# A two-layer hybrid backbone on one Trainium2 core: the state-space part's last step is emitted within the output projection, and its decay rows are asked for two steps ahead

## The chip, the cores and the metric

One NeuronCore of a Trainium2 chip runs the whole program in one launch. The metric is the device time of that core in microseconds, lower is better; beside the timed runs there is one profiled execution, from which every row below is taken.

## The reference

Two layers work on 512 latent tokens and 256 context tokens of width 1024. In each, a modulated RMS norm and an input projection feed three parallel mixers: latent attention, retention and a state-space mixer (SSD). Their outputs, side by side, go through one output projection; then comes a dense feed-forward part (layer 0) or a router with eight experts (layer 1). The last layer gives only the latent tokens. What the change touches is the state-space mixer, for each of 8 heads and both directions:

```
acum = cumsum(log_a)                       # per chunk of 128 tokens
seg = acum[:, None] - acum[None, :]
decay = exp(where(mask, seg, -inf))
scores = (q k^T) * decay
y = scores v                               # within the chunk
state = state * exp(acum[-1]) + (k * w_end)^T v
y += (q * exp(acum)) state_in              # from the chunks before
y = rmsnorm((y + xs * d_skip) * silu(z))
out = concat(att, ret, y) @ w_out
```

## The kernel before, in words

The kernel is written for a tile framework: Python code emits instructions, a scheduler sorts them by priority (the order in which they were emitted, as far as dependences and free buffers let it), and each of the five engines then runs its own list strictly in that order. Tiles come from pools with a fixed number of slots, set in `open_main` (L263): `s2` has 23 slots of 2 KB a partition, `s3` has 30 of 3 KB, `b1` has 4 PSUM tiles of one bank, `w` holds four weight tiles `wraw` of 512 KB each with their high and low parts `whi` and `wlo`. All weight and row transfers are issued by SP, one after the other; an issue waits on SP until its tile is free, and what stands behind it waits too.

The state-space part of a layer is the generator `ssd_run` (L761). It first runs `ssd_states` (L718): the cumulative sums go to DRAM (`cumd`, L725), the chunk states are made (`csps`) and passed on in a scan (`scan_step`, tiles `cs`), with the retention mixer's transposes (`mid`) in between. Then it loops over steps. A step is one chunk of 128 tokens and one of two groups of four heads; layer 0 has 6 chunks, so 12 steps, in the order of chunks 4, 5, 0, 1, 2, 3 (the context first); layer 1 has 4 chunks and 8 steps. For a step,

- `spread` (L780) asks for the decay rows: two transfers (one a direction) of four rows of `cumd`, each copied to all 128 partitions, into two `segE` tiles of `s2`;
- `seg` (L787) subtracts the column sums: eight ScalarE activations of 128x128, four into a PSUM tile `segps` and four in place in `segE`, and VectorE merges them with one predicated copy (L795);
- `weights` (L798) takes the exponential on ScalarE and multiplies with the scores `smask` on VectorE;
- `out` (L803) makes four products `ssdy` on TensorE into the chunk's PSUM tile, eight records in the profile;
- `scores` (L765) for each chunk makes `smask` and the coefficients `cf`; `inter` (L810) for each chunk makes the products `ssdi` with the incoming state, scaled on VectorE (`ssdt`) and added on GpSimd (`ssdu`);
- `final` (L829) adds up a finished chunk and multiplies with the gate `z` (two VectorE operations on `ssdu`); `done` (L1441) takes its square sum on ScalarE, and for every pair of chunks a chain of small VectorE operations (`rq_f`) makes the reciprocal root that scales the pair.

In the loop (L838 to L855) iteration i asks for the rows of step i+1, subtracts for step i, makes the weights of step i-1 and the products of step i-2. The rows of the first step are asked for when the scan is done.

`weave` (L88) emits this generator interleaved with two others by weights: the modulation columns and gates (`mods`: loads `wraw<-in_modw_dram`, products `modps`) and the gate z (`z_run`: products `zps`). The weight of the state-space generator is 22.6 + 5.3 for each chunk (L1457). Behind the weave, `mix_T` (L985) transposes finished chunks by pairs into the projection's operands (`mixps` on TensorE, `mixh` on ScalarE, `mixl` on VectorE), and `wout` (L1464) makes the output projection: for each half of the columns and each 128-token tile 24 products `woutps` (8 slices of the inner dimension, each with three split products) into one `b1` tile, then `x`: a product with the gate and a sum with the residual `xre`. The transposes of the last pair of chunks are emitted within the first half, ahead of the last tile but one (`late`, L1482). What follows is the norm, the feed-forward part (`ffn`, whose `hh`, `hl` and tanh tile `fth` are `s3` tiles like the 16 tiles of its input) or the router and the experts.

Of the kernel before, what the change touches and what calls it, by code (L numbers as in the profile page):

```python
# [255 lines left out]
class Net:  # L256
# [5 lines left out]

    def open_main(self, w=(4, 4, 4), s3=30, s2=23, b2=2, b1=4):  # L263
        tc, ctx = self.tc, self.ctx
# [452 lines left out]

    def ssd_states(self, l, xsT, bmT, mid):  # L718
        pr = self.b2("rowps")
# [20 lines left out]
        yield 5.2  # L740
        yield from mid()
        for cs_, steps in self.SCAN:
            PS = {}
# [17 lines left out]
    def ssd_run(self, l, order, xsT, bmT, cmT, Z, mid, done):  # L761
        IN = yield from self.ssd_states(l, xsT, bmT, mid)
        Wt, SMs, py, fin, R, cf = {}, {}, {}, {}, {}, {}
# [72 lines left out]
        steps = [(c, g) for c in order for g in range(2)]  # L836
        spread(*steps[0])
        scores(order[0])  # L838
        for i, (c, g) in enumerate(steps):
            if i + 1 < len(steps):  # L840
                spread(*steps[i + 1])
            seg(c, g)
            if i:
                weights(*steps[i - 1])
            if g == 1 and i + 1 < len(steps):
                scores(steps[i + 1][0])
            yield 1.0
            if i >= 2:
                out(*steps[i - 2])
                if steps[i - 2][1]:  # L850
                    final(steps[i - 2][0])
                yield 0.9
            if g == 1:
                inter(c)
                yield 0.9  # L855
# [490 lines left out]
    def mixer(self, l, hT, begin, mods, last):  # L1346
# [39 lines left out]
        mixT = self.new_T("mix", 2)  # L1386
# [65 lines left out]
        def late(tl):  # L1452
# [3 lines left out]
        Z = {}  # L1456
        weave((self.ssd_run(l, out_t, xsT, bmT, cmT, Z, ret_mix, done), 22.6 + 5.3 * len(out_t)), (mods, 0.5 if last else 20.0),  # L1457
              (self.z_run(l, hT, out_t, Z), 6.5 * len(out_t)))
        mixT.extend(self.new_T("mix", 4))
        for tl in segt[:-1]:  # L1460
            late(tl)()
        return mixT, late(segt[-1])

    def wout(self, l, mixT, tiles, gates, xin, late, hook, mid=None):  # L1464
# [9 lines left out]
        for h in range(2):  # L1474
# [4 lines left out]
            for i, t in enumerate(tiles):  # L1479
                n = h * len(tiles) + i  # L1480
                load(n + 2)
                if h == 0 and i == len(tiles) - 2:  # L1482
                    late()
                s = 0 if t < 4 else 1
                cs = slice(128 * t, 128 * t + 128)
                ps = self.b1("woutps")
                for k in range(8):
                    o = 512 * (k % 2)
                    self.mm3(ps, (mixT[k][0][:, cs], mixT[k][1][:, cs]),
                             (us[k // 2][0][:, o:o + 512], us[k // 2][1][:, o:o + 512]), k == 0, k == 7)  # L1490
                    if mid and k in (1, 4, 5):
                        mid()
# [704 lines left out]
```

## Time and profile before

| | |
|---|---|
| median of 3 runs | 2031.25 us (2030.02 to 2034.23) |
| the profiled execution | 2027.31 us, its span 2025.5 us |
| mean granted clock of TensorE | 0.965 of full speed |
| TensorE busy | 1888.1 us |
| the state-space stretch of layer 0 | about 355 to 425 us of the span |
| the state-space stretch of layer 1 | about 1320 to 1360 us of the span |

The span is from the first to the last instruction; the execution's own time is 1.8 us more. The engines work side by side, so the busy times don't add up to the span: what counts is which engine stands still in a stretch, and for whom. In the rows, PE is TensorE, PEld its loading of weights, DVE VectorE, ACT ScalarE, POOL GpSimd, SP the engine that issues most transfers. A name like `ssdy<-xst,segE` gives the tile written and those read.

### The profile page before, as it was taken

How to read it: one execution, taken by the hardware profiler on the slowest of the kernel's cores; microseconds unless marked ns; L12 is line 12 of the kernel's file. 1: busy time of each engine (PE TensorE's matmuls, PEld its weight loads, DVE VectorE, ACT ScalarE, POOL GpSimd, SP SyncE). 2: the span in 40 equal slices, each digit the busy share in tenths (PEclk: the TensorE clock that was granted, in tenths of full speed). 3: DMA queues.
4: the chain of work that ended last, by engine and by line, in shares of the span. 5: the costliest groups of instructions: out<-in, count | busy, mean ns of one | idle time of the engine just before them, and what ended most of it. 6: DMA issues, size and time to landing. Idle time of an engine off the chain costs nothing. (4 is left out here: it accounts for less than half of the span.)

```text
span 2025.5 us, 28080 instructions
## 1 busy us (share of the span) xinstructions
PE 1888.1 (93%) x10467; PEld 1549.7 (77%) x10467; DVE 1252.4 (62%) x2470; ACT 832.9 (41%) x1400; POOL 241.7 (12%) x220
## 2 busy tenths in 40 slices
PE   5999999879999999999999999979699889989896
PEld 3777886668888888888887778867588768877774
DVE  5555374667733933833677455775786679659875
ACT  4444223734321220221244442363464467447654
POOL 1100011310003003003002000231210211011001
PEclk9999999989999999999998999979799989999998
DMA  6401115623422711711722011233995799569952
GB/s 242 147 24 35 42 58 193 224 84 105 139 80 70 243 63 53 249 63 61 230 74 88 22 42 63 65 119 116 364 373 172 231 332 335 191 189 364 348 158 72
DMA packets 103208, 310.06 MB, mean 153 GB/s; under 512 B 12171, under 2 KB 19467, under 8 KB 103008
## 3 DMA queue, kind: packets, MB, share of 16 engines
q1 hardware_dynamic: 96320, 290.96, 41.7%
q0 software_dynamic: 6272, 16.43, 2.9%
q8 instruction: 102, 1.67, 0.3%
q14 instruction: 98, 0.80, 0.1%
q10 hardware_dynamic: 416, 0.20, 0.0%
HBM read 293.86 MB, written 14.94 MB: 152 GB/s over the span
## 5 line engine op out<-in xcount | busy, mean ns | idle before, releaser
L309 DVE TENSOR_TENSOR ws<-wr,ws 128x1024 fp32r<-128x1024 f32 (+1 forms) x272 | 319.7, 1191 | 140.2 <-ACT ws L306 120.9
L321 PE MATMUL gups<-ws,xT 128*128 128x512 f32 (+1 forms) x1536 | 349.3, 387 | 26.7 <-issue 18.9
L306 ACT ACTIVATE ws<-wr 128x1024 fp32r<-128x1024 f32 (+1 forms) x272 | 278.8, 1032 | 185.9 <-PE gups L321 106.1
L321 PEld LDWEIGHTS gups<-ws,xT 128*128 128x128 f32 x1536 | 274.6, 192 | 89.1 <-issue 29.0
L306 ACT ACTIVATE whi<-wraw 128x1024 fp32r<-128x1024 f32 x126 | 133.1, 1057 | 493.5 <-PE downps L321 127.7
L309 DVE TENSOR_TENSOR wlo<-wraw,whi 128x1024 fp32r<-128x1024 f32 x123 | 152.8, 1244 | 148.4 <-ACT whi L306 147.7
L321 PE MATMUL dnps<-ws,hTh 128*128 128x512 f32 (+1 forms) x484 | 151.4, 400 | 0.0
L321 PE MATMUL gps<-mixh,whi 128*128 128x256 f32 (+1 forms) x360 | 120.9, 336 | 3.0 <-DVE fth L318 3.0
L321 PE MATMUL gps<-mixl,whi 128*128 128x256 f32 (+1 forms) x360 | 120.9, 336 | 1.2 <-POOL mixl L309 0.7
L321 PE MATMUL gps<-mixh,wlo 128*128 128x256 f32 (+1 forms) x360 | 120.2, 334 | 0.0
L321 PE MATMUL ups<-mixl,whi 128*128 128x256 f32 (+1 forms) x360 | 119.9, 333 | 0.0
L321 PE MATMUL ups<-mixh,whi 128*128 128x256 f32 (+1 forms) x360 | 119.8, 333 | 0.0
L321 PE MATMUL ups<-mixh,wlo 128*128 128x256 f32 (+1 forms) x360 | 119.7, 332 | 0.0
L318 DVE SCALAR_TENSOR_TENSOR junk<-wraw,crow 128x512 bf16<-128x512 f32 x160 | 104.9, 706 | 10.5 <-DMA wraw<-in_modw_dram 10.5
L321 PE MATMUL downps<-whi,hh 128*128 128x512 f32 x264 | 103.7, 393 | 2.0 <-DVE nv L315 2.0
L321 PEld LDWEIGHTS dnps<-ws,hTh 128*128 128x128 f32 (+1 forms) x484 | 88.1, 186 | 21.0
L321 PE MATMUL downps<-wlo,hh 128*128 128x512 f32 x264 | 103.4, 392 | 0.0
L321 PE MATMUL downps<-whi,hl 128*128 128x512 f32 x264 | 103.2, 391 | 0.0
L1955 POOL DMA_INDIRECT yd<-my,dst x20 | 42.6, 2128 | 490.8 <-DVE my L318 463.6
L309 POOL TENSOR_TENSOR x<-x,dtmp 128x512 f32<-128x512 f32 x36 | 50.2, 1396 | 390.0 <-DVE dtmp L309 390.0
L309 DVE TENSOR_TENSOR dtmp<-downps,gate 128x512 f32<-128x512 f32 x48 | 33.0, 690 | 95.2 <-PE downps L321 86.3
L321 PE MATMUL dnps<-ws,hTl 128*128 128x512 f32 x220 | 87.5, 398 | 0.0
(410 smaller groups left out, 4076.7 us busy)
## 6 DMA issues: line engine op xcount, KB each, us to landing
wr<-in_moe_dram SPq DMA_DIRECT2D x248, 512.0 KB, 5.4
wraw<-in_modw_dram SPq DMA_DIRECT2D x94, 512.0 KB, 4.0
wraw<-in_ffn_dram SPq DMA_DIRECT2D x66, 512.0 KB, 3.8
wraw<-in_win_dram SPq DMA_DIRECT2D x44, 512.0 KB, 3.3
segE<-cumd SPq DMA_DIRECT2D x40, 256.0 KB, 4.3
wraw<-in_wout_dram SPq DMA_DIRECT2D x16, 512.0 KB, 3.5
wr<-in_moe_dram POOLq DMA_DIRECT2D x8, 512.0 KB, 15.8
wr<-in_moe_dram SPq DMA_DIRECT2D x16, 256.0 KB, 3.4
```

Of the source, the lines that this page charges most:

```text
L306: return self.nc.scalar.activation(out, in_, func, **kw)
L309: return (eng or self.nc.vector).tensor_tensor(out, a, b, op)
L318: return self.nc.vector.scalar_tensor_tensor(out, a, s, b, op0, op1, accum_out=accum)
L321: return self.nc.tensor.matmul(out, lhsT, rhs, start=start, stop=stop)
L1955: nc.gpsimd.indirect_dma_start(out=self.yd[h], out_offset=bass.IndirectOffsetOnAxis(ap=self.dst[:r, c:c + 1], axis=0), in_=y[b][h][:r], in ...
```

## The change

- `ssd_states` takes a callback that asks for the rows of the first two steps once the retention transposes are emitted, ahead of the scan; in the loop, iteration i asks for the rows of step i+2.
- `inter` of a chunk is emitted at its first step and no longer at its second.
- The generator yields None ahead of its last iteration, and the weave runs it only up to there, with the weight 22.6 + 4.8 for each chunk - 3.0. `mixer` hands the generator on, and `wout` advances it after the third and the sixth slice of each of the first tiles of its first half, and to its end ahead of the last pair's transposes. So the last step's subtraction, the last two steps' weights and products and the last chunk's `final` are emitted between products of the projection.
- `s3` has 29 slots, `s2` has 26.

```diff
--- before.py
+++ after.py
@@ -260,7 +260,7 @@
         self.dp = ctx.enter_context(tc.tile_pool(name="dram", bufs=1, space=DRAM))
         self.zero_made = False
 
-    def open_main(self, w=(4, 4, 4), s3=30, s2=23, b2=2, b1=4):
+    def open_main(self, w=(4, 4, 4), s3=29, s2=26, b2=2, b1=4):
         tc, ctx = self.tc, self.ctx
         self.pools = ExitStack()
         self.cp = self.pools.enter_context(tc.tile_pool(name="cst", bufs=1))
@@ -715,7 +715,7 @@
         i = o.index(c) + 1
         return o[i] if i < 6 else None
 
-    def ssd_states(self, l, xsT, bmT, mid):
+    def ssd_states(self, l, xsT, bmT, mid, spread):
         pr = self.b2("rowps")
         for c in range(6):
             self.tr(pr[:16, 128 * c:128 * c + 128], self.cumS[:, c, :])
@@ -739,6 +739,7 @@
             self.act(self.xst[c], ps)
         yield 5.2
         yield from mid()
+        spread()
         for cs_, steps in self.SCAN:
             PS = {}
             for c in cs_:
@@ -759,7 +760,6 @@
         return IN
 
     def ssd_run(self, l, order, xsT, bmT, cmT, Z, mid, done):
-        IN = yield from self.ssd_states(l, xsT, bmT, mid)
         Wt, SMs, py, fin, R, cf = {}, {}, {}, {}, {}, {}
         later = self.U.bitcast(I32).unsqueeze(1).to_broadcast([128, 4, 128])
 
@@ -834,11 +834,13 @@
             done(c, v)
 
         steps = [(c, g) for c in order for g in range(2)]
-        spread(*steps[0])
+        IN = yield from self.ssd_states(l, xsT, bmT, mid, lambda: [spread(*s) for s in steps[:2]])
         scores(order[0])
         for i, (c, g) in enumerate(steps):
-            if i + 1 < len(steps):
-                spread(*steps[i + 1])
+            if i == len(steps) - 1:
+                yield None
+            if i + 2 < len(steps):
+                spread(*steps[i + 2])
             seg(c, g)
             if i:
                 weights(*steps[i - 1])
@@ -850,7 +852,7 @@
                 if steps[i - 2][1]:
                     final(steps[i - 2][0])
                 yield 0.9
-            if g == 1:
+            if g == 0:
                 inter(c)
                 yield 0.9
         weights(*steps[-1])
@@ -1454,12 +1456,13 @@
         self.g2 = {}
         mods = cat(self.mod_gate(l, 2, (0,) if last else (0, 1), self.g2), *mods)
         Z = {}
-        weave((self.ssd_run(l, out_t, xsT, bmT, cmT, Z, ret_mix, done), 22.6 + 5.3 * len(out_t)), (mods, 0.5 if last else 20.0),
+        ssd = self.ssd_run(l, out_t, xsT, bmT, cmT, Z, ret_mix, done)
+        weave((iter(lambda: next(ssd), None), 22.6 + 4.8 * len(out_t) - 3.0), (mods, 0.5 if last else 20.0),
               (self.z_run(l, hT, out_t, Z), 6.5 * len(out_t)))
         mixT.extend(self.new_T("mix", 4))
         for tl in segt[:-1]:
             late(tl)()
-        return mixT, late(segt[-1])
+        return mixT, (ssd, late(segt[-1]))
 
     def wout(self, l, mixT, tiles, gates, xin, late, hook, mid=None):
         X = {t: [None, None] for t in tiles}
@@ -1480,7 +1483,9 @@
                 n = h * len(tiles) + i
                 load(n + 2)
                 if h == 0 and i == len(tiles) - 2:
-                    late()
+                    for _ in late[0]:
+                        pass
+                    late[1]()
                 s = 0 if t < 4 else 1
                 cs = slice(128 * t, 128 * t + 128)
                 ps = self.b1("woutps")
@@ -1488,6 +1493,8 @@
                     o = 512 * (k % 2)
                     self.mm3(ps, (mixT[k][0][:, cs], mixT[k][1][:, cs]),
                              (us[k // 2][0][:, o:o + 512], us[k // 2][1][:, o:o + 512]), k == 0, k == 7)
+                    if h == 0 and i < len(tiles) - 2 and k % 3 == 2:
+                        next(late[0], None)
                     if mid and k in (1, 4, 5):
                         mid()
                 x = self.s2("x")
```

The orders of the engines differ in the two state-space stretches alone. Three places of layer 0, each before and after (numbers are positions in the engine's list, `x` is a count of equal neighbours, line numbers of the changed kernel are up to 7 higher at the end):

SP, from the first load behind `cumd` on; `segE` are decay rows, two transfers a step, `wraw` the modulation and projection weights. Before:

```order
34 L376 DMA wraw<-in_modw_dram 128x1024 x7
35 L513 DMA gate<-modd_3118 128x4x128 x4
36 L376 DMA wraw<-in_modw_dram 128x1024 x4
37 L785 DMA segE<-cumd_2835 128x512 x6
38 L376 DMA wraw<-in_modw_dram 128x1024 x3
39 L785 DMA segE<-cumd_2835 128x512 x4
40 L376 DMA wraw<-in_modw_dram 128x1024 x3
41 L785 DMA segE<-cumd_2835 128x512 x4
42 L376 DMA wraw<-in_wout_dram 128x1024 x3
43 L785 DMA segE<-cumd_2835 128x512 x4
```

After:

```order
34 L376 DMA wraw<-in_modw_dram 128x1024 x3
35 L785 DMA segE<-cumd_2835 128x512 x4
36 L376 DMA wraw<-in_modw_dram 128x1024 x3
37 L513 DMA gate<-modd_3109 128x4x128 x4
38 L376 DMA wraw<-in_modw_dram 128x1024 x8
39 L785 DMA segE<-cumd_2835 128x512 x4
40 L376 DMA wraw<-in_modw_dram 128x1024
41 L785 DMA segE<-cumd_2835 128x512 x2
42 L376 DMA wraw<-in_modw_dram 128x1024
43 L785 DMA segE<-cumd_2835 128x512 x2
44 L376 DMA wraw<-in_modw_dram 128x1024
45 L376 DMA wraw<-in_wout_dram 128x1024 x3
```

The rows of steps 0 and 1 (`segE` x4) moved from behind seven loads, four gates and four loads to behind three loads; the rows of steps 2 and 3 stand behind 14 modulation loads, where those of steps 3 and 4 stood. Three lines further down the rows of steps 7 to 11 are one run (`segE` x10).

VectorE, where the first pair of latent chunks is scaled (L314, `ssdu` x2) ahead of the projection. Before, from the predicated copy of the last step on:

```order
499 L795 COPY_PREDICATED segE<-cstt,segps 128x512
500 L318 SCALAR_TENSOR_TENSOR rq_f<-rq_f 128x2
501 L309 TENSOR_TENSOR segE<-segE,smask 128x512
502 L309 TENSOR_TENSOR rq_f<-rq_f 128x2
503 L309 TENSOR_TENSOR ssdu<-ssdu,z 128x512
504 L318 SCALAR_TENSOR_TENSOR rq_f<-rq_f,ssd_ss 128x2
505 L309 TENSOR_TENSOR segE<-segE,smask 128x512
506 L318 SCALAR_TENSOR_TENSOR ssd_ss<-rq_f 128x2
507 L309 TENSOR_TENSOR ssdt<-ssdi,ea 128x256
508 L314 TENSOR_SCALAR ssdu<-ssdu,ssd_ss 128x512 x2
509 L309 TENSOR_TENSOR ssdt<-ssdi,ea 128x256 x3
510 L318 SCALAR_TENSOR_TENSOR mixl<-mixps,snh,mixh 128x256
```

After, from the scaling on:

```order
501 L314 TENSOR_SCALAR ssdu<-ssdu,ssd_ss 128x512 x2
502 L318 SCALAR_TENSOR_TENSOR mixl<-mixps,snh,mixh 128x256
503 L309 TENSOR_TENSOR segE<-segE,smask 128x512
504 L309 TENSOR_TENSOR ssdu<-ssdy,ssdu 128x512
505 L318 SCALAR_TENSOR_TENSOR mixl<-mixps,snh,mixh 128x256
506 L309 TENSOR_TENSOR ssdu<-ssdu,z 128x512
507 L318 SCALAR_TENSOR_TENSOR mixl<-mixps,snh,mixh 128x256 x3
508 L795 COPY_PREDICATED segE<-cstt,segps 128x512
509 L309 TENSOR_TENSOR segE<-segE,smask 128x512
510 L309 TENSOR_TENSOR x<-woutps,gate 128x512
511 L309 TENSOR_TENSOR x<-x,xre 128x512
512 L309 TENSOR_TENSOR ssdu<-ssdy,ssdu 128x512
```

The copy of the last step, the multiplies of the last two steps and the sums of the last two chunks (`ssdu<-ssdy,ssdu` and `ssdu<-ssdu,z`) stood ahead of the scaling or right behind it; now they follow it, the last of them between the projection's `x` operations.

TensorE, around the projection's start. Before:

```order
1459 L321 MATMUL ssdy<-xst,segE 128x64 x4
1460 L321 MATMUL ssps<-cmT,bmT 128x128 x2
1461 L321 MATMUL ssdy<-xst,segE 128x64 x4
1462 L321 MATMUL ssdi<-cs,cmT 128x512 x4
1463 L321 MATMUL ssdy<-xst,segE 128x64 x12
1464 L331 MATMUL mixps<-ident,ssdu 128x128 x2
1465 L321 MATMUL ssdy<-xst,segE 128x64 x4
1466 L331 MATMUL mixps<-ident,ssdu 128x128 x14
1467 L321 MATMUL woutps<-whi,mixh 128x512
```

After:

```order
1462 L321 MATMUL ssdy<-xst,segE 128x64 x4
1463 L321 MATMUL ssdi<-cs,cmT 128x512 x2
1464 L321 MATMUL ssdy<-xst,segE 128x64 x4
1465 L331 MATMUL mixps<-ident,ssdu 128x128 x8
1466 L321 MATMUL ssdy<-xst,segE 128x64 x4
1467 L331 MATMUL mixps<-ident,ssdu 128x128 x8
1468 L321 MATMUL woutps<-whi,mixh 128x512
```

The transposes `mixps` of the first pairs now stand between the products of steps 8 and 9 and behind those, and the last two steps' `ssdy` are gone from here. The first of them stands within the projection, behind 33 of its products:

```order
1499 L321 MATMUL woutps<-wlo,mixh 128x512
1500 L321 MATMUL woutps<-whi,mixl 128x512
1501 L321 MATMUL ssdy<-xst,segE 128x64 x4
1502 L321 MATMUL woutps<-whi,mixh 128x512
1503 L321 MATMUL woutps<-wlo,mixh 128x512
```

Nine products further on comes the last one.

## Rows read from the trace of the kernel before

**Rows 1.** The page, busy time of the engines over the span: us, share, instructions.

```profile
PE 1888.1 (93%) x10467; PEld 1549.7 (77%) x10467; DVE 1252.4 (62%) x2470; ACT 832.9 (41%) x1400; POOL 241.7 (12%) x220
```

**Rows 2.** Busy time by stretches, layer 0: length, each engine's busy us, granted clock, DMA share, GB/s.

```profile
355.00:425.00 70.00, 51.12 (x316) 38.16 (x314) 53.15 (x130) 50.23 (x138) 23.93 (x26) 0.83 0.63 213
375.00:425.00 50.00, 34.52 (x205) 26.88 (x205) 42.48 (x104) 36.10 (x97) 20.01 (x22) 0.80 0.62 201
425.00:450.00 25.00, 24.59 (x113) 20.46 (x113) 11.19 (x30) 6.18 (x18) 0.00 (x0) 1.00 0.06 22
```

**Rows 3.** Timeline of TensorE, layer 0: start, length, instruction, count, [idle before, releaser].

```profile
404.20 1.10 PE L321 MATMUL ssdy<-xst,segE 128*128 128x64 f32 x8 [1.03 <-DVE segE L309]
410.72 1.97 PE L321 MATMUL ssdy<-xst,segE 128*128 128x64 f32 x8 [5.42 <-DVE segE L309]
417.20 1.97 PE L321 MATMUL ssdy<-xst,segE 128*128 128x64 f32 x8 [4.51 <-DVE segE L309]
...
425.41 0.47 PE L321 MATMUL woutps<-whi,mixh 128*128 128x512 f32 x1 [1.05 <-DVE mixl L318]
```

**Rows 4.** Timeline of VectorE, layer 0.

```profile
366.64 0.72 DVE L795 COPY_PREDICATED segE<-cstt,segps 128x512 f32<-128x512 int32 x1
...
374.98 0.72 DVE L795 COPY_PREDICATED segE<-cstt,segps 128x512 f32<-128x512 int32 x1
...
413.24 0.71 DVE L795 COPY_PREDICATED segE<-cstt,segps 128x512 f32<-128x512 int32 x1
...
415.79 0.71 DVE L795 COPY_PREDICATED segE<-cstt,segps 128x512 f32<-128x512 int32 x1
...
417.82 0.67 DVE L309 TENSOR_TENSOR segE<-segE,smask 128x512 f32<-128x512 f32 x1
...
422.89 0.69 DVE L309 TENSOR_TENSOR ssdu<-ssdy,ssdu 128x512 f32<-128x512 f32 x1 [0.24 <-POOL ssdu L309]
```

**Rows 5.** Timeline of SP, layer 0; a length takes in the waits of the counted issues.

```profile
349.71 3.02 SPq L785 DMA_DIRECT2D segE<-cumd  x6
352.83 12.66 SPq L376 DMA_DIRECT2D wraw<-in_modw_dram  x3
366.20 1.83 SPq L785 DMA_DIRECT2D segE<-cumd  x4
```

**Rows 6.** Timeline of ScalarE, layer 0.

```profile
355.41 1.18 ACT L306 ACTIVATE segps<-segE,sj 128x128 f32<-128x128 f32 x3 [5.20 <-DMA segE<-cumd]
```

**Rows 7.** The tile segE, both layers: what its instructions waited for, us, times.

```profile
  DMA segE<-cumd: 11.0, 7
```

**Rows 8.** Busy time by stretches, layer 1.

```profile
1320.00:1360.00 40.00, 28.30 (x160) 23.85 (x159) 31.22 (x74) 31.37 (x91) 15.65 (x18) 0.77 0.33 114
```

**Rows 9.** Timeline of TensorE, layer 1.

```profile
1326.15 0.80 PE L321 MATMUL ssps<-cmT,bmT 64*128 64x128 f32 x4 [4.68 <-ACT smask L306]
...
1356.49 1.97 PE L321 MATMUL ssdy<-xst,segE 128*128 128x64 f32 x8 [2.73 <-DVE segE L309]
...
1360.04 0.78 PE L321 MATMUL woutps<-whi,mixh 128*128 128x512 f32 x1
```

**Rows 10.** Timeline of ScalarE, layer 1.

```profile
1320.22 0.60 ACT L306 ACTIVATE z<-zps 128x512 f32<-128x512 f32 x1 [7.37 <-PE zps L321]
```

**Rows 11.** Groups of instructions, 350 to 426: shapes, count, busy us, mean ns, idle before.

```profile
L306 ACT ACTIVATE segps<-segE,sj 128x128 f32<-128x128 f32 x48 | 17.2, 359 | 9.2 <-DMA segE<-cumd 7.1 <-DVE rq_f L309 1.5 <-DVE segE L795 0.3
L309 POOL TENSOR_TENSOR ssdu<-ssdu,ssdt 128x256 f32<-128x256 f32 x20 | 16.6, 841 | 22.1 <-DVE ssdt L309 17.3 <-DVE rq_f L314 2.3 <-DVE modc L318 1.8
L306 ACT ACTIVATE segE<-segE,sj 128x128 f32<-128x128 f32 x48 | 15.8, 388 | 3.9 <-DMA segE<-cumd 3.9
...
L306 ACT ACTIVATE segE<-segE 128x512 f32<-128x512 f32 x12 | 7.5, 622 | 4.9 <-DVE segE L795 2.6 <-DVE rq_f L318 2.3
```

**Rows 12.** Timeline of VectorE, feed-forward part of layer 0.

```profile
542.69 0.95 DVE L318 SCALAR_TENSOR_TENSOR hl<-fth,hh 128x768 fp32r<-128x768 f32 x1
```

**Rows 13.** Timeline of ScalarE, feed-forward part of layer 0.

```profile
549.78 0.79 ACT L306 ACTIVATE fth<-gps 128x768 f32<-128x768 f32 x1
```

## The prediction

> **What bounds the kernel now.** I read the page first: TensorE is busy 1888.1 us, 93% of the span [rows 1], so over the whole program a microsecond only counts where TensorE stands still. Then the busy time by stretches, to find where it does. In layer 0's state-space part, 355 to 425 us, TensorE has 51.12 us of work in 70.00, at a granted clock of 0.83, that is between its two levels of 1.2 and 2.4 GHz; right behind, from 425 to 450, it is busy 24.59 of 25.00 at 1.00 [rows 2]. So the stage holds about 19 us of idle TensorE plus a slow clock, and what follows is bound by TensorE: a microsecond saved ahead of the first output projection is a microsecond of the run.
>
> What TensorE waits for is in the chain of its own instructions: late in the stage each group of state-space products (ssdy) stands behind the VectorE multiply that finishes the decay weights (segE): 1.03, 5.42 and 4.51 us, and the first projection product (woutps) starts at 425.41 [rows 3]. From 375 to 425 VectorE is busy 42.48 of 50 us and ScalarE 36.10 [rows 2]. The predicated copies, one a step, show the pace: step 3 at 374.98, step 10 at 413.24 [rows 4], so 38.26 us for 7 steps, 5.47 each. VectorE is the nearly full engine of the second half; in the first half it is not: 53.15 of 70 us over the stage less 42.48 of 50 leaves 10.67 us in the first 20 [rows 2].
>
> There the reason is the queue. SP issues the decay rows of steps 0 to 2 at 349.71, ScalarE's first use of them starts at 355.41 after 5.20 us of waiting for the transfer [rows 5, 6]; then SP stands 12.66 us in three modulation loads, and only at 366.20 come the rows of steps 3 and 4 [rows 5]. All waits for the rows' transfers in the program, 7 of them and all ScalarE's in this stage, are 11.0 us [rows 7]. Layer 1 has the same picture in 40 us: TensorE 28.30 busy at clock 0.77, VectorE 31.22, ScalarE 31.37 [rows 8]; TensorE waits 4.68 us for ScalarE at 1326.15 and 2.73 us for VectorE at 1356.49, and the first woutps is at 1360.04 [rows 9]; ScalarE in its turn waited 7.37 us, in order, on a z product before it could begin with step 0 [rows 10].
>
> **The change, term by term.** The sum is made against the profiled execution, 2027.31 us, which is 3.94 below the median of the runs, 2031.25; I add that at the end.
>
> *Early rows.* Rows of steps 0 and 1 are asked ahead of the scan. The first order excerpt shows them behind 3 loads instead of 15, so the 5.20 us wait of ScalarE [rows 6] goes; half of each step (the four activations that need no PSUM tile) stands ahead of the last scan step. But the price stands in the same excerpt: rows of steps 2 and 3 now follow 14 modulation loads, as steps 3 and 4 did, so step 2 may be no earlier than before (366.64 [rows 4]). What gains is step 3, asked together with step 2: one step of pace, less what ScalarE needs to work it off. Eight activations of 0.36 and 0.39 us and the exponential of 0.62 [rows 11] are 3.6 us a step. I put step 3's copy at about 370 instead of 374.98: 5 us (bounds 0, if the loads hold it as now, and 8.3, if it comes right behind step 2's place).
>
> *Tail behind the start.* What the second excerpt shows going from ahead of the first projection to between its tiles is, on VectorE, the copy of step 11 (0.71), the two multiplies of steps 10 and 11 (0.67 each) and four adds and products of the last two chunks (0.69 each) [rows 4]: 0.71 + 2 x 0.67 + 4 x 0.69 = 4.81 us. On TensorE the two ssdy groups of steps 10 and 11 move into the projection (third excerpt; the second of them follows nine products later). At full clock 8 records take 1.10 us [rows 3], so 2.2 us are given back.
>
> *Pace.* From step 3 to the projection VectorE had 42.48 us in 50 [rows 2]; less 4.81 it is 37.7. Starting at 370, fully packed, the projection could start at 370 + 37.7 = 407.7; at the 85% that it reaches now, at 370 + 44.4 = 414.4. Two things argue for the upper half of that packing: rows two steps ahead end most of the 11.0 us of waits [rows 7], and the inter-chunk products one step earlier give GpSimd's adds (0.84 us each [rows 11]) more time. Against it: the rsqrt chain of the first pair stays in order among larger operations. I take 410: 425.41 - 410 = 15.4, less 2.2 is 13.2 us for layer 0.
>
> *Layer 1.* Here rows were already asked ahead of need in a block; now steps 0 and 1 precede the other loads, and ScalarE can fill the 7.37 us wait [rows 10]. After 1320 ScalarE has 31.37 us to do [rows 8]. Less eight early activations (8 x 0.37 = 3.0) and less the last step's eight and two exponentials (3.0 + 1.2) [rows 11] are 24.2; at 31.37/40 packing that is 30.8 us, at full packing 24.2, so the projection could start between 1344 and 1351. I take 1350, because the pair's rsqrt chain and the transposes stand at the end whatever ScalarE does. That is 10.0, less 1.1 for one more ssdy group within the projection (the other is there already): 8.9 us.
>
> *Pools.* One 3 KB tile fewer, three 2 KB tiles more. In the feed-forward part the need is 16 + 12 + 1 = 29 tiles, and the single tanh tile is free in time: its last reader ends at 542.69 + 0.95 = 543.64, and it is written again at 549.78 [rows 12, 13]; 6.1 us of cover. I cost it at nothing, within 2 us either way; without the cover, 22 such tiles would each wait. Outside the two stretches the orders are the same.
>
> Sum: 13.2 + 8.9 = 22.1 us. 2027.31 - 22.1 = 2005.2; with 3.94, **2009 us**. The terms that I am unsure of are the pace (407.7 to 414.4 is 6.7 us) and layer 1's start (7 us); the forecast's own range is 2002 to 2017.
>
> **The rivals.** *The rows are no further ahead than before where it counts.* The change asks two ahead, but SP works in order, and in layer 0 the requests of steps 2 to 6 are still strung between weight loads that wait for TensorE. Then step 3 gains 5 us, the pace stays at 5.47 a step up to step 10, which comes at 370 + 38.3 = 408.3 instead of 413.24; behind it the first pair's scaling follows as before. Layer 0 gains 4.9 and some 3 of the tail's 4.81, less 2.2; layer 1 half of its 8.9: together 10, that is 2021. For it: the 12.66 us block [rows 5]. Against: further down in SP's order the rows of steps 7 to 11 stand as one run of ten requests.
>
> *Everything packs to the engines' floors.* Layer 0 starts projecting at 404 (step 3 at 366.6, 37.7 behind), layer 1 at 1344: gains of 19.2 and 14.9, 1997. VectorE's small operations take up to 1 us among the large ones now, which speaks against it.
>
> *The moved step becomes the wait, and the kernel gets slower.* The place is tile 1 of the projection. VectorE's order (second excerpt) puts copy and multiply of step 11 ahead of the first tile's gate product x; ssdy, segps and the projection share four PSUM tiles, so if step 11's rows are late, x is late, and TensorE stops within the projection, where today it runs without a pause. Price: one block of SP as long as today's longest, 12.66 us [rows 5], in each layer is 25.3, more than the 22.1 gained; with about 1 us of slow clock behind each stop (1.97 against 1.10 us for the same 8 records [rows 3]) it would be 2031.25 - 22.1 + 27.3 = 2036. It decides from a lateness of some 11 us a layer. Against it: rows of step 11 were copied at 415.79 and multiplied at 417.82 [rows 4], and from 410 the projection has two tiles of 24 products, at 24.59 us for 113 [rows 2] 10.4 us, before it needs a third PSUM tile, that is until 420; so they would have to come later than today.
> On that order the Trainium skill, PSUM — Partial Sum Buffer, section Engine vs sequencer instructions, says that ScalarE's and VectorE's queues are strictly first in, first out. By that rule x could not pass a late copy, and the full 12.66 would be paid; the trace agrees as far as it goes, in ScalarE's 7.37 us behind one z [rows 10].
> The same skill, TensorE: Matmul & The Clock Gate, section HAM oscillation, says that pauses between bursts put the array back to half rate each time. By it a stop would cost its matmuls twice; the trace agrees: behind the 5.42 us wait the same 8 records took 1.97 us instead of 1.10 [rows 3].
>
> *Gain and loss cancel*: half of the rival's stop in both layers against a partial gain, 2027 to 2035.
>
> **How the numbers follow.** A measurement of this kernel tells about 0.2%, 4 us, from no change. Chances: forecast 0.60, rows no further ahead 0.20, engines' floors 0.05, cancelling 0.08, slower by the late last step 0.07. The predicted time is the forecast's, 2009. The range of 8 in 10 takes the forecast whole and reaches over the second case to 2026, and down to 2000 for half of the floors' case. Faster by over 0.2% is forecast, second and third case, 0.85; the same 0.08; slower 0.07.
>
> **What would show it.** Right: ScalarE's waits for decay rows, 11.0 us now, near 2; copies of steps 3 to 10 at 4 to 4.7 us a step; first woutps near 410, and near 1337 in layer 1 (1350 less layer 0's 13.2); the two ssdy groups within the projection without idle time ahead. Wrong: SP waiting 10 us at a modulation load with rows queued behind; idle TensorE time ahead of a woutps; a TensorE wait in the feed-forward part for the tanh tile. If the first woutps comes where I say and the total does not follow, something behind takes it back, and my claim that the rest is bound by TensorE is the one that fails.

## The result, and the profile after

The changed kernel takes 2045.8 us (median of 6 runs, 2043.73 to 2047.95), the kernel before 2032.24 (6 runs): the ratio is 1.007, with a 95% interval of 1.0048 to 1.0092. It is slower, by some 14 us; the forecast was 2009. The profiled execution took 2046.38 us, its span is 2044.6.

The page of the changed kernel, first line of the busy times, to set beside [rows 1]: TensorE has 11 us more to do (slower products, not more of them) and its share is the same.

```profile
PE 1899.2 (93%) x10467; PEld 1555.3 (76%) x10467; DVE 1253.3 (61%) x2470; ACT 832.3 (41%) x1400; POOL 239.0 (12%) x220
```

Busy time by stretches, layer 0, the same three as in [rows 2]: over 355 to 425 TensorE takes 54.77 us for its work, at a clock of 0.79 and not 0.83, and VectorE is busy 51.76 us and not 53.15; from 425 on TensorE is full, as before.

```profile
355.00:425.00 70.00, 54.77 (x317) 39.70 (x317) 51.76 (x138) 45.75 (x125) 23.47 (x26) 0.79 0.55 183
375.00:425.00 50.00, 36.51 (x204) 27.31 (x204) 41.93 (x108) 34.25 (x94) 18.50 (x20) 0.74 0.53 175
425.00:450.00 25.00, 25.00 (x122) 20.96 (x121) 12.58 (x30) 6.63 (x19) 0.00 (x0) 0.98 0.18 64
```

The scan, the steps and the projection of layer 0 stand as follows. VectorE first: the last three scan operations (cs) and the predicated copies of steps 2, 3, 9 and 10, to set beside [rows 4].

```profile
358.43 0.76 DVE L309 TENSOR_TENSOR cs<-csps,sct 128x256 f32<-128x256 f32 x2 [5.71 <-PE csps L321]
...
360.25 0.41 DVE L309 TENSOR_TENSOR cs<-csps,sct 128x256 f32<-128x256 f32 x1
...
370.91 0.73 DVE L795 COPY_PREDICATED segE<-cstt,segps 128x512 f32<-128x512 int32 x1 [3.07 <-ACT segps L306]
...
384.85 0.73 DVE L795 COPY_PREDICATED segE<-cstt,segps 128x512 f32<-128x512 int32 x1 [0.47 <-ACT segps L306]
...
409.41 0.72 DVE L795 COPY_PREDICATED segE<-cstt,segps 128x512 f32<-128x512 int32 x1
...
416.67 0.71 DVE L795 COPY_PREDICATED segE<-cstt,segps 128x512 f32<-128x512 int32 x1
```

The last scan operation of the kernel before:

```profile
350.99 0.42 DVE L309 TENSOR_TENSOR cs<-csps,sct 128x256 f32<-128x256 f32 x1
```

The scan waits 5.71 us for its products (csps), its last operation stands at 360.25, before at 350.99. Step 3 is copied at 384.85, not 374.98; but from there to step 10 it is 416.67 - 384.85 = 31.82 us for 7 steps, 4.55 each, where it was 5.47.

Between steps 2 and 3 ScalarE waits 3.05 us for rows and 2.68 us for a modulation product.

```profile
378.40 1.28 ACT L306 ACTIVATE segE<-segE,sj 128x128 f32<-128x128 f32 x4 [3.05 <-DMA segE<-cumd]
382.37 0.77 ACT L306 ACTIVATE segps<-segE,sj 128x128 f32<-128x128 f32 x2 [2.68 <-PE modps L321]
```

All waits for the rows' transfers, to set beside [rows 7], are 7.3 us; the forecast had them near 2:

```profile
  DMA segE<-cumd: 7.3, 8
```

SP, layer 0, to set beside [rows 5]: the rows of steps 0 and 1 are asked at 328.75 as meant; then eight modulation loads take 20.38 us, the rows of steps 2 and 3 follow at 361.66, those of step 6 at 382.23.

```profile
328.75 1.85 SPq L785 DMA_DIRECT2D segE<-cumd  x4
...
341.19 20.38 SPq L376 DMA_DIRECT2D wraw<-in_modw_dram  x8
361.66 3.61 SPq L785 DMA_DIRECT2D segE<-cumd  x4
...
382.23 2.98 SPq L785 DMA_DIRECT2D segE<-cumd  x2
```

TensorE at the start of the projection, to set beside [rows 3]: it waits 7.04 us for the scaled chunks (ssdu, L314) and starts at 424.81, 0.6 us earlier than before. The last two ssdy groups stand in the projection without idle time ahead, as meant.

```profile
423.03 2.12 PE L331 MATMUL mixps<-ident,ssdu 128*128 128x128 f32 x8 [7.04 <-DVE ssdu L314]
424.81 0.78 PE L321 MATMUL woutps<-whi,mixh 128*128 128x512 f32 x1
...
433.02 1.00 PE L321 MATMUL ssdy<-xst,segE 128*128 128x64 f32 x8
...
436.00 1.00 PE L321 MATMUL ssdy<-xst,segE 128*128 128x64 f32 x8
```

Layer 1, VectorE and then TensorE, to set beside [rows 8 to 10]: the scan waits twice for its products, for 4.04 and 2.25 us. The projection starts at 1368.22 after a wait of 5.97; and within it, behind the last ssdy at 1381.91, TensorE stands idle for 1.51 and 1.25 us ahead of two of the router's operations and then for 2.40 us ahead of the last pair's transposes, whose scaled chunks are late. What follows runs at a granted clock of 0.50, the lower level, up to 1395.5.

```profile
1322.73 0.42 DVE L309 TENSOR_TENSOR cs<-csps,sct 128x256 f32<-128x256 f32 x1 [4.04 <-PE csps L321]
...
1328.21 0.76 DVE L309 TENSOR_TENSOR cs<-csps,sct 128x256 f32<-128x256 f32 x2 [2.25 <-PE csps L321]
```

```profile
1366.44 2.12 PE L331 MATMUL mixps<-ident,ssdu 128*128 128x128 f32 x8 [5.97 <-DVE ssdu L314]
1368.22 0.78 PE L321 MATMUL woutps<-whi,mixh 128*128 128x512 f32 x1
...
1381.91 1.00 PE L321 MATMUL ssdy<-xst,segE 128*128 128x64 f32 x8
...
1385.87 0.66 PE L331 MATMUL rtps<-ident,x 128*128 128x128 f32 x4 [1.51 <-DVE x L309]
1387.78 1.06 PE L321 MATMUL lgtp<-rta,rv 128*128 128x8 f32 x8 [1.25 <-ACT rv L306]
1391.24 0.66 PE L331 MATMUL mixps<-ident,ssdu 128*128 128x128 f32 x2 [2.40 <-DVE ssdu L314]
```

Busy time and granted clock of TensorE in the stretch behind it:

```profile
1391.24:1395.50 4.26, 4.26 (x14) 0.50 0.00 0
```

### The profile page after: what moved, and what is told of

Read it like the earlier page. It is cut to its first block, busy times and chain, and to the rows that moved or that the text cites. A ratio compares the mean times of both kernels' runs of the same rounds, so it can differ in the third digit from the quotient of the medians.

```text
span 2044.6 us, 28050 instructions
## 1 busy us (share of the span) xinstructions
PE 1899.2 (93%) x10467; PEld 1555.3 (76%) x10467; DVE 1253.3 (61%) x2470; ACT 832.3 (41%) x1400; POOL 239.0 (12%) x220
## 5 line engine op out<-in xcount | busy, mean ns | idle before, releaser
L318 DVE SCALAR_TENSOR_TENSOR junk<-wraw,crow 128x512 bf16<-128x512 f32 x160 | 104.9, 705 | 10.4 <-DMA wraw<-in_modw_dram 10.4
```

The source lines that it names most:

```text
L318: return self.nc.vector.scalar_tensor_tensor(out, a, s, b, op0, op1, accum_out=accum)
```

## The experiments

All kernels are the changed one or the one before with the edits named. Theory W says that the smaller weight of the state-space generator sorts z products ahead of the scan; L that the late last step costs time within the projection; R that rows stand behind weight loads. The table gives the median, the ratio to the kernel before with its interval, and from the profiled execution the last scan operation on VectorE, the first woutps and the first product of the feed-forward part (layer 0); the last three columns are layer 1's last scan operation, first woutps and first product after the router, all counted from layer 0's end in the same execution, so that the two layers can be read apart. These six columns come from one execution of each kernel, while the times of one kernel's runs lie 3 to 15 us apart: a difference of a few us in a column is weak by itself. (A merged row's start stands for the last scan operation where it is merged with its neighbour.)

| kernel | median us | ratio (95%) | scan 0 | wout 0 | end 0 | scan 1 | wout 1 | end 1 |
|---|---|---|---|---|---|---|---|---|
| before | about 2031 | 1 | 351.0 | 425.4 | 497.0 | 821 | 863 | 929 |
| changed | 2045.8 | 1.007 (1.0048 to 1.0092) | 360.2 | 424.8 | 500.5 | 830 | 868 | 942 |
| changed, old weight | 2026.46 | 0.9973 (0.996 to 0.9986) | 352.1 | 415.1 | 490.7 | 822 | 858 | 932 |
| before, new weight | 2036.53 | 1.0019 (1.0004 to 1.0034) | 360.9 | 431.8 | 504.9 | 829 | 869 | 932 |
| changed, slower z | 2026.89 | 0.9987 (0.9973 to 1.0001) | 353.5 | 415.0 | 490.1 | 821 | 858 | 931 |
| changed, not late | 2036.78 | 1.0024 (1.0006 to 1.0042) | 359.1 | 424.9 | 498.1 | 830 | 865 | 932 |
| old weight, not late | 2013.29 | 0.99 (0.987 to 0.9931) | 351.5 | 415.9 | 487.5 | 821 | 859 | 922 |
| old weight, late but sooner | 2015.88 | 0.9932 (0.991 to 0.9954) | 351.7 | 414.9 | 490.4 | 822 | 858 | 924 |
| before, rows ahead | 2018.32 | 0.9925 (0.9903 to 0.9946) | 351.5 | 419.4 | 494.5 | 821 | 853 | 920 |
| before, inter early | 2024.09 | 0.9968 (0.995 to 0.9985) | 352.2 | 424.5 | 499.0 | 820 | 859 | 925 |
| before, rows and inter | 2018.61 | 0.9947 (0.9929 to 0.9966) | 351.7 | 417.7 | 490.3 | 822 | 860 | 924 |
| not late, weight 6.0 | 2011.71 | 0.99 (0.9866 to 0.9933) | 353.7 | 414.4 | 488.9 | 824 | 857 | 922 |
| not late, weight 7.0 | 2002.1 | 0.9854 (0.9813 to 0.9895) | 348.8 | 407.6 | 482.4 | 819 | 852 | 919 |
| old weight, not late, fewer loads | 2023.69 | 0.9967 (0.9946 to 0.9987) | 351.2 | 423.2 | 496.4 | 821 | 860 | 923 |

**The weight.** The old weight in the changed kernel:

```diff
-        weave((iter(lambda: next(ssd), None), 22.6 + 4.8 * len(out_t) - 3.0), (mods, 0.5 if last else 20.0),
+        weave((iter(lambda: next(ssd), None), 22.6 + 5.3 * len(out_t)), (mods, 0.5 if last else 20.0),
```

> The changed kernel with only the interleaving weight of the state-space generator put back (22.6 + 5.3 a chunk, where the change has 22.6 + 4.8 a chunk - 3.0). Theory W, that the smaller weight sorts z products ahead of the scan and so starts the chain of steps late (last scan step of layer 0 at 358.4 instead of 349 us, of layer 1 some 9 us late as well): the scans come back to about 349 in layer 0, the first woutps come 8 to 9 us earlier in each layer, and the time is 2028 to 2034. Rival L, that the late last step within the projection costs the time: the first woutps may move, the stops within the projection stay, and the time is 2038 to 2046. Rival R, that rows two ahead stand behind weight loads: the copy of step 3 in layer 0 stays near 385 and the time above 2040.

Measured 2026.46 us, 19 less than the changed kernel and 5 less than the one before; W had expected 2028 to 2034, so it gained a little more than that. The last scan operation of layer 0 is back at 352.1, the projection starts 9.8 us earlier, in layer 1 some 10. Step 3 is copied at 370.15, which is the prediction's 370. Rivals L and R fall as the main cause; what L names is still there (below).

The new weight in the kernel before (the same edit the other way round):

> The kernel before with only the new weight. Theory W: the last scan step of layer 0 moves from 349 to about 357, the first woutps of both layers come 6 to 9 us later, and the time is 2042 to 2050. Rivals L and R: the chain of steps has slack ahead of it, the time stays within 4 us of 2032.

Measured 2036.53 us. The scan moves as W says, and the projection starts 6.4 us later in layer 0 and 6 in layer 1. VectorE, layer 0, shows the same wait ahead of the last scan steps as the changed kernel:

```profile
359.44 0.42 DVE L309 TENSOR_TENSOR cs<-csps,sct 128x256 f32<-128x256 f32 x1 [5.61 <-PE csps L321]
```

But the time rises by only 4.7 us (1 to 7 by the interval); W expected 10 at least, so its size alone is a miss. The two profiled executions are 12.5 us apart (2039.8, the slowest of its ten, against 2027.31), so they can't settle where the rest goes.

To tell z products from modulation products, whose standing to the state-space generator the weight moves as well, only the z generator's weight was scaled back:

```diff
-              (self.z_run(l, hT, out_t, Z), 6.5 * len(out_t)))
+              (self.z_run(l, hT, out_t, Z), 6.5 * len(out_t) * (19.6 + 4.8 * len(out_t)) / (22.6 + 5.3 * len(out_t))))
```

> The changed kernel with the weight of the z generator scaled so that the two generators stand to each other as before (the state-space weight and everything else as changed). If it is z products sorted ahead of the scan that theory W is about, the last scan steps come back to about 352 and 1312 us and the time to 2024 to 2032, as with the old weight (2026.46). If it is the modulation loads and products, whose weight stands to the state-space generator as in the change here, layer 0 stays late (last scan step near 360) and the time is over 2036.

Measured 2026.89 us, the same as with the old weight. The modulation weight stands as in the change, and the loads ahead of the rows of step 2 still come as a block; it is merely shorter (SP, layer 0; 20.38 us for eight in the changed kernel). That TensorE frees their tiles sooner fits, but no row here shows it:

```profile
337.99 13.14 SPq L376 DMA_DIRECT2D wraw<-in_modw_dram  x7
```

The trace also shows the z products themselves. Ahead of the scan's last products (csps, at 348.7 in the kernel before and 357.3 in the changed one) TensorE has done 96 of them before and 126 after (busy time of the tile zps alone, from 318 to there, before and then changed):

```profile
318.00:348.70 30.70, 12.74 (x96) 11.80 (x96) 1.58 (x3) 1.20 (x2) 1.00 0.54 188
```

```profile
318.00:357.30 39.30, 16.57 (x126) 15.44 (x126) 1.05 (x2) 0.60 (x1) 1.00 0.62 215
```

By the same count it is 120 with the new weight alone and 96 with the old weight or the slower z. The modulation products ahead of the same place are 53 before, 63 in the changed kernel and 65 with the slower z, where the scan is early all the same. So it is the z products: W stands, R falls as a cause of its own. The late scan and the late rows of steps 2 and 3 come and go together in these runs; which of the two holds step 3 is not separated.

**The late last step.** Taken out of the changed kernel (the generator runs to its end in the weave, and `wout` only transposes the last pair):

```diff
-            if i == len(steps) - 1:
-                yield None
...
-                    if h == 0 and i < len(tiles) - 2 and k % 3 == 2:
-                        next(late[0], None)
```

> The changed kernel with the last step emitted in the weave again, ahead of the projection; all else as changed. Theory L: the stops within the first half of layer 1's projection (5 us of idle TensorE and about 5 us at half clock around 1383 to 1393) go, the projection starts 2 to 5 us later in each layer, and the time is 2036 to 2041. Theory W alone: the projection starts later and nothing is won behind it, 2046 to 2052.

Measured 2036.78 us, 9 less. But the projection does not start later without it: 424.85 against 424.81 in layer 0, and in layer 1 2.5 us sooner after layer 0's end. The late step won nothing at the start even there.

With both put back, weight and last step:

> The changed kernel with two parts put back: the old weight and the last step in the weave; left are the rows two steps ahead, the earlier inter-chunk products and the pools. Theories W and L as separate costs: with the old weight the projections start as in the run with the old weight alone (415.05 and 1348.48 us) or up to 3 us later, and the first projection takes 71 instead of 74.2 us, layer 1's 59 instead of 66.7; the time is 2014 to 2020. If the late step only costs where the chain starts late (an interaction), the time stays at 2024 to 2029.

Measured 2013.29 us: 13 less than with the late step, 18 less than before. Weight and late step are separate costs, and the sum is a little more than W and L expected. In layer 1 the transposes of the last pair come at 1359.26 without idle time, between the products of the second tile and those of the third:

```profile
1359.26 1.04 PE L331 MATMUL mixps<-ident,ssdu 128*128 128x128 f32 x8
```

The same step late, but its pieces one after each of the first five slices of the first tile:

```diff
-                    if h == 0 and i < len(tiles) - 2 and k % 3 == 2:
+                    if h == 0 and i == 0 and k < 5:
```

> The changed kernel with the old weight, and the last step's pieces within the projection after each of the first five slices of its first tile, so that in layer 1 the last products of the state-space part stand behind 14 products of the projection and not behind 39 or more. Theory L, in the form that the late step costs because the last pair's sums, its root and its transposes have too little work left ahead of them: layer 1's idle time of 2.4 and 1.5 and 1.25 us and the half-clock products behind them go, layer 0 changes by less than 2 us, and the time is 2016 to 2021 (2026.46 with the old weight, 2013.29 with the step in the weave). Rival: whatever is emitted within the projection delays its first tiles by PSUM tiles and VectorE's order: 2023 to 2030.

Measured 2015.88 us: 10.6 of the 13 us come back. The last ssdy of layer 1 stands at 1353.72, 5.7 us behind the projection's start, and TensorE no longer waits for the pair:

```profile
1351.67 1.00 PE L321 MATMUL ssdy<-xst,segE 128*128 128x64 f32 x8
...
1353.72 1.00 PE L321 MATMUL ssdy<-xst,segE 128*128 128x64 f32 x8
```

So it is not the step within the projection as such that costs, nor VectorE's order ahead of x: it is what follows on it. Behind the last ssdy come a sum and the product with z, the square sum, the root's chain, two scalings, eight transposes and their split before the third tile can start. In the changed kernel VectorE begins the sum at 1383.02 and scales at 1390.61, 7.6 us, and TensorE has six projection products and the router's to do meanwhile.

```profile
1383.02 0.69 DVE L309 TENSOR_TENSOR ssdu<-ssdy,ssdu 128x512 f32<-128x512 f32 x1 [5.98 <-PE ssdy L321]
...
1390.61 0.88 DVE L314 TENSOR_SCALAR ssdu<-ssdu,ssd_ss 128x512 f32<-128x512 f32 x2
```

**Rows ahead, inter-chunk products, pools.** On the kernel before, the rows two steps ahead alone (`spread` of the first two steps ahead of the scan, `steps[i + 2]` in the loop):

> The kernel before with the decay rows alone asked two steps ahead (pools as before). By the prediction's terms, early rows and pace without the tail: first woutps of layer 0 at 413 to 420 instead of 425.41, layer 1 some 5 us earlier, 2015 to 2023. Rival R, rows stand behind weight loads anyway: within 4 us of 2032.

Measured 2018.32 us, 13 less than before, within what was expected; the projection of layer 0 starts at 419.4. Rival R falls again. From step 3 to 10 it takes 405.37 - 366.49 = 38.88 us, 5.55 a step: the rows alone bring step 3 forward by 8.5 us but not the pace. (The late last step alone on the kernel before gave no time: that kernel deadlocks. What the step costs there is not known.)

The inter-chunk products alone (`if g == 1` to `if g == 0`):

> The kernel before with only the inter-chunk products emitted at a chunk's first step. Without the rows ahead it should change little: within 4 us of 2032. If the adds on GpSimd were what holds the sums of a finished chunk, 2024 to 2028.

Measured 2024.09 us: 7 less, the rival's figure. The trace does not place it: layer 0 ends 2 us later (499.0), layer 1 is 3 us shorter. It was not followed further, and on top of the rows it is gone:

> The kernel before with the rows two steps ahead and the earlier inter-chunk products, the pools as before (30 tiles of 3 KB, 23 of 2 KB). Against the run with these two and the new pools (2013.29) it shows the pools. If three more 2 KB tiles are what lets rows be asked early: 2017 to 2021. If they change nothing: within 3 us of 2013.3.

Measured 2018.61 us, as the rows alone. Against the run with the new pools (2013.29) that is 5 us for three more 2 KB tiles and one 3 KB tile fewer, or 9.5 by the two ratios (0.9947 and 0.99); their intervals (0.9929 to 0.9966, 0.987 to 0.9931) just touch, so a worth of nothing is not excluded, and it could be more than 9.5.

So the change builds up like this: before about 2031, rows 2018.3, with inter-chunk products 2018.6, with pools 2013.3, with the late step 2026.5, with the new weight 2045.8.

**Further along.** If a small weight loses, a larger one may gain. The last step in the weave, 6.0 and then 7.0 a chunk:

> The changed kernel with the last step in the weave and a larger weight, 22.6 + 6.0 a chunk. Theory W carried on: the scan comes still earlier than with the old weight, the z products move behind it and fill TensorE's gaps between the steps; 3 to 8 us under the run with the old weight and the last step in the weave. Rival: with the old weight the scan no longer waits for z products, the time is within 3 us of that run, or z products come so late that the finished chunks wait for them, 3 to 10 us over it.

Measured 2011.71 us, within 3 us of the run with the old weight, as the rival had it.

> The changed kernel with the last step in the weave and the weight 22.6 + 7.0 a chunk. The run with 6.0 a chunk (2011.71) stood within 3 us of that with 5.3 (2013.29): theory W then says that scans no longer wait for z products, and this one is within 3 us of 2012 too. If z products now come too late for the finished chunks, 2015 to 2025.

Measured 2002.1 us, 29 less than the kernel before and the fastest of all; both expectations missed. Its z products reach to the last steps: 24 each at 390.21 and 393.99, ahead of the last four and the last three ssdy groups, where the run with the old weight has its last 48 z products from 386.37 to 392.2 and six groups to come. The scan is earlier too (348.8 and 819). The order is not monotone in the weight: with 6.0 the scan came at 353.7 and 824. TensorE stands idle less between the steps. What the earlier scan and what the later z products are worth was not separated. The stretch 340 to 415 of layer 0, with the old weight and then with 7.0:

```profile
340.00:415.00 75.00, 65.43 (x416) 47.14 (x416) 56.31 (x153) 46.64 (x130) 24.32 (x30) 0.89 0.61 207
```

```profile
340.00:415.00 75.00, 69.92 (x463) 51.02 (x462) 61.17 (x170) 51.02 (x138) 24.70 (x29) 0.95 0.72 239
```

TensorE is busy 69.92 of 75 us and not 65.43, at a granted clock of 0.95 and not 0.89, VectorE 61.17 and not 56.31.

Fewer modulation loads ahead of the rows (their weight 14, not 20):

> The changed kernel with the old weight and the last step in the weave (2013.29), and the weight of the modulation generator 14 and not 20, so that the rows of steps 0 to 8 stand behind fewer modulation loads on SP, and those loads and their products later. If rows behind loads (rival R) still hold layer 0: copies of steps 3 to 8 come 2 to 5 us earlier and the time is 2008 to 2011. If VectorE's own work sets the pace by now: within 3 us of 2013.3, or up to 6 us over it where the projection's first weights, now behind all rows, come too late.

Measured 2023.69 us, 10 more, over both expectations. The copies of steps 3 to 5 do come 4.4 to 6.2 us earlier, but step 8 comes 1.4 us later and the projection 7.3. The loads that no longer stand ahead of the rows stand behind them: up to 418.69 TensorE waits 4.75 us for a modulation row, in order, ahead of the first pair's transposes; ScalarE makes that row only behind a square sum for which it waited 3.91 us. TensorE, then ScalarE:

```profile
418.69 1.11 PE L331 MATMUL modps<-ident,modrow 128*128 128x128 f32 x4 [4.75 <-ACT modrow L306]
```

```profile
417.43 0.63 ACT L306 ACTIVATE junk<-ssdu 128x512 bf16<-128x512 f32 x1 [3.91 <-DVE ssdu L309]
...
418.06 0.58 ACT L306 ACTIVATE modrow<-modps 128x512 f32<-128x512 f32 x1
```

The Trainium skill, PSUM — Partial Sum Buffer, section Engine vs sequencer instructions, has ScalarE's queue strictly first in, first out; these rows agree.

## Why the prediction was wrong, point by point

- *What bounds the kernel.* Right where nothing was moved into the projection: where the projection started 9.5 us earlier in layer 0 (old weight, not late), that layer also ended 9.5 us earlier, and the whole gained 18.
- *Early rows, step 3 at 370.* Measured 384.85, and 370.15 with the old weight. The term was sound, but the step failed in what it left out, and this is the main failure: the change also lowers a weight, and I gave that no term. It put the scan 9 us later in both layers (360.2 for 351.0, 830 for 821) behind z products, and SP's eight loads ahead of the rows of step 2 took 20.38 us. It cost 19 us with the late step and 23 without.
- *Pace.* 4.55 us a step from step 3 to 10, within the forecast's 4 to 4.7, but by luck: step 3 stood 10 us late. Where it stands at 370 as forecast (old weight), step 10 is at 404.19: 4.86 a step. My first reason, the rows two steps ahead, gave 5.55 alone; with the earlier inter-chunk products it is 4.95.
- *Projection of layer 0 at 410.* Measured 424.81, and 415.05 with the weight put back: 0.65 us past the end of the forecast's own range (407.7 to 414.4). The two ssdy groups within it cost what was said: 96 products, the two groups and the start take 449.18 - 424.81 = 24.4 us for 447.30 - 425.41 = 21.9.
- *Tail behind the start.* This step failed second. I let 4.81 us of VectorE's work move behind the start and gained them in full. The start moved by 0.9 us in layer 0 (415.91 to 415.05) and 1 in layer 1: what it waits for is the first pair's root chain, scaling and transposes. Two of the moved operations, 1.4 of the 4.81 us (at 422.89 and 424.19), stood behind that scaling already in the kernel before. The others stood between the operations of the chain, and with the late step other work of VectorE stands there instead (splits of weights, `wlo`, and of transposes, `mixl`), so that the scaling comes only 0.7 us sooner. The scaling in the kernel before, then with the old weight, not late and late:

```profile
418.82 1.34 DVE L314 TENSOR_SCALAR ssdu<-ssdu,ssd_ss 128x512 f32<-128x512 f32 x2
```

```profile
413.35 0.87 DVE L314 TENSOR_SCALAR ssdu<-ssdu,ssd_ss 128x512 f32<-128x512 f32 x2
```

```profile
412.65 0.87 DVE L314 TENSOR_SCALAR ssdu<-ssdu,ssd_ss 128x512 f32<-128x512 f32 x2
```

- *Layer 1, 1.1 us for one more group.* Of the terms that the sum has, this cost most: with the old weight the projection there, from its start to the first product behind the router, took 73.8 us with the late step and 63.4 without, 10.4 us. I looked at the moved group's own length and not at what waits for it. The slower rival had the place (within the projection, a stop at the cost of the clock) and, for layer 1, nearly the price, 12.66 us a layer; in layer 0 the stretch from the start of the projection to its end grew by 4.1 us. Its reason, late rows that hold x, was not what happened. The last pair's chain was late, and only in layer 1, where two tiles lie ahead of that pair; layer 0 has four.
- *Pools at nothing.* A gain of 5 us by the medians, with nothing not excluded; I had allowed 2.
- What stays open: why the weight costs 19 to 23 us with the rows ahead and 4.7 (1 to 7) without them, though the scan moves as far.

## What to carry to other kernels

Where a table of weights or due times interleaves two streams, a changed weight is a moved block of work: price it as such, by the first instruction of the chain that now stands behind the other stream, before any term for what the change is about. A step that is moved behind the start of the next phase must be priced by whoever waits for its end: count the work that remains between its new place and that consumer against the whole chain in between, for each layer with its own number of tiles. And what fills the gaps of a chain may be worth keeping for the chain's end: the fastest kernel here differs from the one with the old weight and the step in the weave only in the weight, and by it the chain starts 3 us earlier and the filler reaches to its last steps.

## What the runs showed of the hardware

One and the same wait cost two different amounts. In all kernels TensorE waits 2.0 us for VectorE ahead of the last 48 products of layer 0's projection. In four of them (before, old weight and not late, rows and inter, slower z) these took 11.15 to 11.16 us; in the other ten 12.7 to 12.8. TensorE's timeline of the runs with the old weight, not late and late, shows the difference: the products take 0.39 us in the one, and in the other eight of them, from the fifth on, 0.63, and the granted clock falls to 0.60 over that stretch, where it stays at 1.00 in the first.

```profile
475.27 0.47 PE L321 MATMUL woutps<-whi,mixh 128*128 128x512 f32 x1 [2.00 <-DVE nv L315]
...
477.19 0.39 PE L321 MATMUL woutps<-whi,mixl 128*128 128x512 f32 x1
```

```profile
477.00:481.00 4.00, 4.00 (x19) 3.34 (x18) 3.83 (x14) 1.51 (x3) 0.74 (x1) 1.00 0.00 0
```

```profile
476.87 0.47 PE L321 MATMUL woutps<-whi,mixh 128*128 128x512 f32 x1 [1.99 <-DVE nv L315]
...
478.31 0.63 PE L321 MATMUL woutps<-whi,mixl 128*128 128x512 f32 x1
```

```profile
478.30:482.00 3.70, 3.70 (x12) 2.88 (x11) 3.56 (x14) 1.58 (x3) 0.73 (x1) 0.60 0.00 0
```

So 1.6 us of difference between two kernels stood behind an equal pause; what decides whether the clock falls there is not shown. Here it makes up part of the 4 us by which the changed kernel's layer 0 takes longer from its projection's start to its end.
